# Transfer sizes and the gamma broadcast in a fused RMSNorm and swish kernel

## The chip, the core and the metric

The kernel runs on one core of one Trainium2 chip. The metric is the device time of the kernel in microseconds, the median over runs; less is better.

## The reference

```
def reference(x, gamma, eps):            # x: 16 x 1024 x 512 float32, gamma: 512
    rms = np.sqrt(np.mean(x ** 2, axis=-1, keepdims=True) + eps)
    x_norm = x / rms * gamma
    return (x_norm * (1.0 / (1.0 + np.exp(-x_norm)))).astype(np.float32)
```

Each of 16,384 rows of 512 numbers is divided by its root mean square, multiplied by gamma, and put through swish. 33.55 MB are read and as many written.

## The kernel before

The input is seen as 128 "rows per partition" of 512 numbers: 128 x 128 rows, and a row of all 128 partitions is 256 KB. A tile is a block of consecutive rows of the input, `sz` rows to each partition, so that each partition reads one run of `sz` x 2 KB from memory. The list `sizes` says how the 128 rows are cut into tiles. The tiles lie in one ring buffer `xb` of 96 rows per partition; the results are written over the input in the ring and are stored from there. A load that takes a place in the ring for the second time has to wait until the store of what lay there has landed.

The computation goes by chunks of `cn` = 4 rows (32 chunks in all), in a software pipeline written out by hand (`tc.manual_schedule()`: each engine runs its instructions in the order of the program):

- `sums(k)`: the sum of squares of each row, three rows on ACT (line 80), one on DVE (line 86).
- `root(k)`: mean plus eps on DVE (line 93), to the power -0.5 on POOL (line 97).
- `norm(k)`: row times its reciprocal root times gamma, four instructions on DVE (line 104).
- `swish(k)`: one ACT instruction over the chunk (line 111).

In turn k of the loop the order is `sums(k)`, `root(k)`, the stores whose last chunk was put through swish in turn k - 1 or before, `norm(k - 1)`, `swish(k - 2)`, and then the loads that have come due. So a chunk's swish stands on ACT behind the sums of two later chunks, and a tile's store behind the sums of its last chunk plus three.

Loads (line 70) are all issued from SP, in order, and nothing else is; 32 rows' worth of tiles is issued ahead of the loop. Stores (line 73) are issued from ACT's queue, between its activations. The framework gives every transfer one of eight completion semaphores in turn, and a transfer that gets a semaphore for the second time is issued only when the earlier transfer on it has landed.

Gamma is needed on all 128 partitions by `norm`. It is brought to partitions 0, 32, 64 and 96 by one transfer from ACT's queue into `gamma4` (line 116), which POOL has set to zero before (line 114), and a DVE shuffle (line 140) copies it within each group of 32 partitions into `gamma_sb`. The shuffle stands on DVE behind `root(0)`.

Of the kernel before, what the change touches and what calls it, by code (L numbers as in the profile page):

```python
# [1 line left out]

# [4 lines left out]


@with_exitstack
def kernel(  # L10
    ctx: ExitStack,
    tc: tile.TileContext,
    x: bass.AP,
    gamma: bass.AP,
    eps: bass.AP,
    out: bass.AP,
):
    nc = tc.nc
    P = nc.NUM_PARTITIONS
    AF = mybir.ActivationFunctionType  # L20
    ALU = mybir.AluOpType
    fp32 = mybir.dt.float32
    bf16 = mybir.dt.bfloat16

    xf = x.flatten_outer_dims()
    of = out.flatten_outer_dims()
    R, D = xf.shape


    sizes = [4, 4, 8] + [16] * 6 + [8, 8]  # L30
    ring = 96
    ahead = 32
    cn = 4
    n_act = 3
    N = sum(sizes)
    assert N * P == R, (N, R)


    tiles = []
    done = 0  # L40
    for sz in sizes:
        assert done % ring + sz <= ring
        tiles.append((done * P, sz, done % ring))
        done += sz
    chunks = [r for _, sz, at in tiles for r in range(at, at + sz, cn)]
    K = len(chunks)

    pool = ctx.enter_context(tc.tile_pool(name="all", bufs=1))
    junk_pool = ctx.enter_context(tc.tile_pool(name="junk", bufs=1))
    xb = pool.tile([P, ring, D], fp32, name="xb")  # L50
    gamma4 = pool.tile([P, D], fp32, name="gamma4")
    gamma_sb = pool.tile([P, D], fp32, name="gamma_sb")
    neg_half = pool.tile([P, cn], fp32, name="neg_half")
    ms = pool.tile([P, K, cn], fp32, name="ms")
    aeps = pool.tile([P, K, cn], fp32, name="aeps")
    rstd = pool.tile([P, K, cn], fp32, name="rstd")

    inv_d = 1.0 / float(D)
    eps_f = float(eps)

    def dram(ap, t):
        first, sz, _ = tiles[t]
        return ap[first : first + P * sz].rearrange("(p n) d -> p n d", n=sz)

    def buf(t):
        _, sz, at = tiles[t]
        return xb[:, at : at + sz, :]

    def load(t):
        nc.sync.dma_start(out=buf(t), in_=dram(xf, t))  # L70

    def store(t):
        nc.scalar.dma_start(out=dram(of, t), in_=buf(t))

    def sums(k):
        for j in range(cn):
            row = xb[:, chunks[k] + j, :]
            if j < n_act:
                junk = junk_pool.tile([P, D], bf16, name=f"junk_a{j}")
                nc.scalar.activation(  # L80
                    out=junk[:], in_=row, func=AF.Square,
                    accum_out=ms[:, k, j : j + 1],
                )
            else:
                junk = junk_pool.tile([P, D], bf16, name=f"junk_v{j}")
                nc.vector.tensor_tensor_reduce(  # L86
                    out=junk[:], in0=row, in1=row,
                    scale=1.0, scalar=0.0, op0=ALU.mult, op1=ALU.add,
                    accum_out=ms[:, k, j : j + 1],
                )  # L90

    def root(k):
        nc.vector.tensor_scalar(  # L93
            out=aeps[:, k, :], in0=ms[:, k, :], scalar1=inv_d, scalar2=eps_f,
            op0=ALU.mult, op1=ALU.add,
        )
        nc.gpsimd.tensor_tensor(  # L97
            out=rstd[:, k, :], in0=aeps[:, k, :], in1=neg_half[:], op=ALU.pow
        )

    def norm(k):
        for j in range(cn):
            row = xb[:, chunks[k] + j, :]
            nc.vector.scalar_tensor_tensor(  # L104
                out=row, in0=row, scalar=rstd[:, k, j : j + 1],
                in1=gamma_sb[:], op0=ALU.mult, op1=ALU.mult,
            )

    def swish(k):
        rows = xb[:, chunks[k] : chunks[k] + cn, :]  # L110
        nc.scalar.activation(out=rows, in_=rows, func=AF.Silu)  # L111

    with tc.manual_schedule():
        nc.gpsimd.memset(gamma4[:], 0.0)  # L114
        nc.gpsimd.memset(neg_half[:], -0.5)  # L115
        nc.scalar.dma_start(out=gamma4[0:P:32, :], in_=gamma.partition_broadcast(4))
        nc.scalar.preload_act_table_set("silu_and_others")  # L117

        loaded = 0
        rows_loaded = 0  # L120
        while rows_loaded < ahead:
            load(loaded)
            rows_loaded += tiles[loaded][1]
            loaded += 1

        ends = []
        e = 0
        for _, sz, _ in tiles:
            e += sz // cn
            ends.append(e)  # L130
        stored = 0
        for k in range(K + 3):
            if k < K:
                sums(k)
                root(k)
            while stored < len(tiles) and ends[stored] <= k - 2:
                store(stored)
                stored += 1
            if k == 0:
                nc.vector.stream_shuffle(gamma_sb[:], gamma4[:], [0] * 32)  # L140
            if 1 <= k <= K:
                norm(k - 1)
            if 2 <= k < K + 2:
                swish(k - 2)
                while loaded < len(tiles) and ends[loaded] <= k - 1 + ahead // cn + 2:
                    load(loaded)
                    loaded += 1


# [1 line left out]
_INS = ['x', 'gamma', 'eps']  # L151
_OUTS = [((16, 1024, 512), 'float32')]

_NUMBERS = {'eps': 9.999999747378752e-06}


# [26 lines left out]
```

## Time and profile before

| | us |
|---|---|
| Median of 3 runs (lowest, highest) | 163.08 (162.92, 163.41) |
| The profiled execution's own time | 162.92 |
| Its span in the trace | 161.1 |
| ACT busy | 118.7 (74% of the span) |
| DVE busy | 110.7 (69%) |
| POOL busy | 46.4 (29%) |
| Load queue (q1), time of its packets as a share of 16 engines | 49.1% |
| Store queue and gamma (q10), the same | 48.4% |

The span is the time from the first to the last instruction of the program in the trace; the time of a run has 1.8 us more around it. Queue q1 is that of the loads from SP, q10 that of ACT. A transfer is cut into packets, one for each run of memory, which are spread over the 16 DMA engines; the trace has a record of every packet with its queue, start, duration and size. Packets of 4 bytes are the completion marks, one for each DMA engine that takes part. The share of a queue is the sum of its packets' durations over 16 times the span.

### The profile page before, as it was taken

How to read it: one execution, taken by the hardware profiler on the slowest of the kernel's cores; microseconds unless marked ns; L12 is line 12 of the kernel's file. 1: busy time of each engine (PE TensorE's matmuls, PEld its weight loads, DVE VectorE, ACT ScalarE, POOL GpSimd, SP SyncE). 2: the span in 40 equal slices, each digit the busy share in tenths (PEclk: the TensorE clock that was granted, in tenths of full speed). 3: DMA queues.
4: the chain of work that ended last, by engine and by line, in shares of the span. 5: the costliest groups of instructions: out<-in, count | busy, mean ns of one | idle time of the engine just before them, and what ended most of it. 6: DMA issues, size and time to landing. Idle time of an engine off the chain costs nothing.

```text
span 161.1 us, 612 instructions
## 1 busy us (share of the span) xinstructions
DVE 110.7 (69%) x226; ACT 118.7 (74%) x225; POOL 46.4 (29%) x38
## 2 busy tenths in 40 slices
DVE  0376946998999999999966998069999604990000
ACT  3447919999999999999939996099999408954000
POOL 1052403333444433333333333033333302400000
DMA  5999989999899999999999999999999999999993
GB/s 171 437 435 521 390 352 488 413 403 480 366 407 431 484 411 447 399 456 447 399 447 456 399 439 464 417 415 421 431 435 464 419 403 472 415 415 423 439 415 146
DMA packets 3180, 67.15 MB, mean 417 GB/s; under 512 B 356, under 2 KB 356, under 8 KB 360
## 3 DMA queue, kind: packets, MB, share of 16 engines
q1 hardware_dynamic: 1584, 33.56, 49.1%
q10 hardware_dynamic: 1592, 33.56, 48.4%
q14 instruction: 4, 0.03, 0.0%
HBM read 33.56 MB, written 33.55 MB: 417 GB/s over the span
## 4 chain that ended last, share of the span: by engine, by line
DMA 59%; ACT 20%; another core or an unknown queue 4%; issue 4%; DVE 3%; SPq 1%; DVEq 0%; ACTq 0%
DMA xb<-in_x_dram 41%; DMA out_dram<-xb 19%; ACT junk_a L80 12%; ACT xb L111 8%; DVE xb L104 3%; SPq L70 1%; DVEq L178 0%; DVE aeps L93 0%; ACTq L80 0%
## 5 line engine op out<-in xcount | busy, mean ns | idle before, releaser
L104 DVE SCALAR_TENSOR_TENSOR xb<-xb,rstd,gamma_sb 128x512 f32<-128x512 f32 x128 | 87.4, 745 | 0.0
L80 ACT ACTIVATE junk_a<-xb 128x512 bf16<-128x512 f32 x96 | 59.0, 615 | 23.9 <-DMA xb<-in_x_dram 23.9
L97 POOL TENSOR_TENSOR rstd<-aeps,neg_half 128x4 f32<-128x4 f32 x32 | 45.6, 1426 | 94.1 <-DVE aeps L93 94.1
L111 ACT ACTIVATE xb<-xb 128x2048 f32<-128x2048 f32 x32 | 60.7, 1896 | 1.8 <-DVE xb L104 1.8
L86 DVE CUSTOM_DVE_ANT_0 junk_v<-xb 128x512 bf16<-128x512 f32 x32 | 21.9, 685 | 19.6 <-DMA xb<-in_x_dram 19.6
L80 ACT ACTIVATION_READ_ACCUMULATOR junk_a<-xb 128x1 f32 x96 | 18.0, 187 | 0.0
L93 DVE TENSOR_SCALAR aeps<-ms 128x4 f32<-128x4 f32 x32 | 5.4, 170 | 14.5 <-ACT junk_a L80 14.5
L117 ACT ACT_TABLE_LOAD x1 | 1.3, 1283 | 2.4 <-issue 2.4
L86 DVE DVE_READ_ACCUMULATOR2_ANT ms<- 128x1 f32 x32 | 2.6, 82 | 0.0
L140 DVE STREAM_SHUFFLE gamma_sb<-gamma 128x512 f32<-128x512 f32 x1 | 0.7, 725 | 0.0
L114 POOL MEMSET gamma<- 128x512 f32 x1 | 0.5, 524 | 0.3 <-POOLq L164 0.3
L164 POOL MEMSET const-float32-0.0<- 128x1 f32 x1 | 0.1, 98 | 0.2 <-issue 0.2
L164 POOL MEMSET const-bfloat16-1.0<- 128x1 bf16 x1 | 0.1, 101 | 0.0
L164 POOL MEMSET const-uint8-127<- 128x1 uint8 x1 | 0.1, 101 | 0.0
L115 POOL MEMSET neg_half<- 128x4 f32 x1 | 0.1, 101 | 0.0
L164 POOL MEMSET const-float32-1.0<- 128x1 f32 x1 | 0.1, 98 | 0.0
L140 DVE LOAD_MASK_SELECT gamma_sb<-gamma x1 | 0.0, 14 | 0.0
## 6 DMA issues: line engine op xcount, KB each, us to landing
xb<-in_x_dram SPq DMA_DIRECT2D x6, 4096.0 KB, 43.8
out_dram<-xb ACTq DMA_DIRECT2D x6, 4096.0 KB, 34.6
xb<-in_x_dram SPq DMA_DIRECT2D x3, 2048.0 KB, 38.8
out_dram<-xb ACTq DMA_DIRECT2D x3, 2048.0 KB, 13.9
xb<-in_x_dram SPq DMA_DIRECT2D x2, 1024.0 KB, 5.8
out_dram<-xb ACTq DMA_DIRECT2D x2, 1024.0 KB, 19.7
gamma<-in_gamma_dram ACTq DMA_DIRECT2D x1, 8.0 KB
```

The costliest lines, as they stand in the source:

```text
L70: nc.sync.dma_start(out=buf(t), in_=dram(xf, t))
L80: nc.scalar.activation(out=junk[:], in_=row, func=AF.Square, accum_out=ms[:, k, j : j + 1],)
L86: nc.vector.tensor_tensor_reduce(out=junk[:], in0=row, in1=row, scale=1.0, scalar=0.0, op0=ALU.mult, op1=ALU.add, accum_out=ms[:, k, j : j ...
L93: nc.vector.tensor_scalar(out=aeps[:, k, :], in0=ms[:, k, :], scalar1=inv_d, scalar2=eps_f, op0=ALU.mult, op1=ALU.add,)
L97: nc.gpsimd.tensor_tensor(out=rstd[:, k, :], in0=aeps[:, k, :], in1=neg_half[:], op=ALU.pow)
L104: nc.vector.scalar_tensor_tensor(out=row, in0=row, scalar=rstd[:, k, j : j + 1], in1=gamma_sb[:], op0=ALU.mult, op1=ALU.mult,)
L111: nc.scalar.activation(out=rows, in_=rows, func=AF.Silu)
L114: nc.gpsimd.memset(gamma4[:], 0.0)
L115: nc.gpsimd.memset(neg_half[:], -0.5)
L117: nc.scalar.preload_act_table_set("silu_and_others")
L140: nc.vector.stream_shuffle(gamma_sb[:], gamma4[:], [0] * 32)
L164: nc = _bacc.Bacc("TRN2", target_bir_lowering=False, num_devices=1)
```

## The change

Two things are changed. The list of tile sizes becomes two tiles of 4 rows (1 MB) and fifteen of 8 rows (2 MB); it was 4, 4, 8, six of 16 (4 MB), 8, 8. The ring, the chunks, the rows loaded ahead of the loop and the code of the loop stay. There are then 17 loads and 17 stores, where there were 11 of each. And gamma goes from memory to all 128 partitions by one transfer on ACT's queue, at the place of the former one; the buffer `gamma4`, its clearing on POOL and the shuffle on DVE are gone.

```
-    sizes = [4, 4, 8] + [16] * 6 + [8, 8]
+    sizes = [4, 4] + [8] * 15
...
-    gamma4 = pool.tile([P, D], fp32, name="gamma4")
...
-        nc.gpsimd.memset(gamma4[:], 0.0)
         nc.gpsimd.memset(neg_half[:], -0.5)
-        nc.scalar.dma_start(out=gamma4[0:P:32, :], in_=gamma.partition_broadcast(4))
+        nc.scalar.dma_start(out=gamma_sb[:], in_=gamma.partition_broadcast(P))
...
-            if k == 0:
-                nc.vector.stream_shuffle(gamma_sb[:], gamma4[:], [0] * 32)
```

## The prediction

> **What bounds the kernel now.** I read the page first: the DMA row of the 40 slices and the shares of the queues, then the chain.
>
> ```profile
> span 161.1 us, 612 instructions
> DVE 110.7 (69%) x226; ACT 118.7 (74%) x225; POOL 46.4 (29%) x38
> DMA  5999989999899999999999999999999999999993
> DMA packets 3180, 67.15 MB, mean 417 GB/s; under 512 B 356, under 2 KB 356, under 8 KB 360
> q1 hardware_dynamic: 1584, 33.56, 49.1%
> q10 hardware_dynamic: 1592, 33.56, 48.4%
> DMA 59%; ACT 20%; another core or an unknown queue 4%; issue 4%; DVE 3%; SPq 1%; DVEq 0%; ACTq 0%
> ```
>
> The two queues together take 97.5% of 16 engines' span, 157.1 of 161.1 us; ACT, the busiest engine, has 42 us to spare. The other 4.0 us lie mainly at the ends. Two kinds of window show it, and what packet size does:
>
> ```profile
> 0.00:1.70 1.70, 0.00 (x0) 0.00 (x0) 0.77 (x6) 1.00 0.00 0
> 60.00:100.00 40.00, 35.27 (x72) 36.67 (x71) 14.49 (x11) 1.00 1.00 433
> 133.20:140.40 7.20, 5.17 (x12) 6.67 (x14) 2.24 (x2) 1.00 1.01 437
> 150.10:155.00 4.90, 0.00 (x0) 0.00 (x0) 0.00 (x0) 1.00 1.00 428
> 159.90:161.10 1.20, 0.00 (x0) 0.00 (x0) 0.00 (x0) 1.00 0.00 0
> ```
>
> The last two columns are the busy share of the DMA engines and GB/s. Nothing moves before 1.7 us and after 159.9; with loads and stores mixed (60 to 100) the share is 1.00. While stores alone run, 4 MB transfers (32 KB packets) pass 437/1.01 = 433 GB/s, 2 MB ones (16 KB packets) 428. So the time is the work in the DMA engines plus some 3 us, and whatever an engine does earlier or later costs nothing as long as one queue has work. The waits of SP say the same:
>
> ```profile
> SPq L70 <- DMA out_dram<-xb: 55.9, 3, 27.1
> SPq L70 <- DMA xb<-in_x_dram: 19.6, 3, 15.3
> ```
>
> Loads were issued 75 us late in sum, for a place in the ring or a semaphore, and the engines were full all the same.
>
> **The work in packets.** The packet records have these medians: 9 ns for a 4-byte mark, 84 ns for 2 KB, 309 for 8 KB, 611 for 16 KB, 1213 for 32 KB. They follow each other without a gap on an engine. Each of 16 engines gets 8 packets and one mark of every transfer. Before, for each queue: 16 x 0.309 (two tiles of 4 rows) + 24 x 0.611 + 48 x 1.213 + 11 x 0.009 = 77.93 us; twice that, and 0.09 for gamma on four engines, is 155.9. The page's 157.1 has 1.2 us more: packets longer than the median, of which 0.4 us are in the first load, 0.5 at 19.5 to 22.9 us, where the first store's data begin (20.9), and 0.2 at 47.
>
> **Smaller tiles.** After, for each queue: 16 x 0.309 + 120 x 0.611 + 17 x 0.009 = 78.42 us. That is 0.49 more; for two queues +0.97 us. The reason is that two 16 KB packets take 1222 ns where one of 32 KB takes 1213, 96 times on each engine (0.86), and 12 more marks (0.11). Bounds: the windows above put it at 433/428, about 1%, of the some 117 us now spent in 32 KB packets, 1.3 us; taken as 433 against 431, which the rounding allows, 0.5. I take the packet medians, which rest on hundreds of packets. A gain is excluded here unless the longer packets go away; they may by up to 0.8 us (those after the first load), or one more start like that at 20 us may add 0.5.
>
> The Trainium skill, "DMA: Bandwidth & Descriptors", section "Anatomy of one DMA", speaks harder against the change: a fixed cost of about 2.0 us for a transfer, most of it waiting for the receipt. Paid in series, 12 more transfers would cost an estimated 24 us, and the sum would be 187 us. The trace disagrees for queued transfers: the marks of the last store but one came from 153.49 to 155.02 us, and in the window from 150.10 to 155.00, where the engines go over to the last store one by one, the share is 1.00; so a receipt is waited for beside the next transfer's data.
>
> **Gamma.** The four packets of 2 KB (360 less 356 in the page's counts) become 128. If they spread like a load's, that is 8 on each engine: 8 x 0.084 + 0.009 = 0.68 us, where engines 0 to 3 or their like had 0.09: +0.6 us, and it is in front of nothing that could hide it, since the loads fill the engines from 1.7 us on. Bounds: the four old packets read the same 2 KB at nearly the same time (starts 5.54 to 5.61) and each took 84 ns, so I take 84; sixteen readers may be slower, at most like an 8 KB packet, 8 x 0.309 = 2.5 us (+2.4). All on four engines, as before, would be 32 x 0.084 = 2.7 us (+2.6). Nothing is the lower bound, if the engine that ends last gets none.
>
> Who waits for it: `norm(0)` on DVE. Before:
>
> ```profile
> 7.52 0.17 DVE L93 TENSOR_SCALAR aeps<-ms 128x4 f32<-128x4 f32 x1 [1.28 <-ACT junk_a L80]
> 7.63 0.72 DVE L140 STREAM_SHUFFLE gamma_sb<-gamma 128x512 f32<-128x512 f32 x1
> 8.25 0.67 DVE L86 CUSTOM_DVE_ANT_0 junk_v<-xb 128x512 bf16<-128x512 f32 x1
> 10.15 2.73 DVE L104 SCALAR_TENSOR_TENSOR xb<-xb,rstd,gamma_sb 128x512 f32<-128x512 f32 x4
> 12.98 0.63 ACT L80 ACTIVATE junk_a<-xb 128x512 bf16<-128x512 f32 x1 [2.94 <-DMA xb<-in_x_dram]
> ```
>
> The first gamma packet moved at 5.54 us. Eight packets in turn with the load's of 0.309 to 0.611 us end at 5.54 + 8 x 0.084 + 7 x 0.309 + 0.611, about 9.0, and land some 0.4 later; `norm(0)` begins at 10.15, behind `root(1)`, and the load before it comes 0.6 us later too. So it waits for nothing new, and if it did, DVE's next work (12.92, with the third load) has little behind it: until 20.9 us only loads move. The shuffle (0.72 us on DVE), the clearing (0.52 on POOL) and the dependence on them save nothing for the same reason: `norm(0)` follows `root(1)` at 10.07, whatever the shuffle does. ACT's issue of the transfer (1.09 us before, at 1.29) lies ahead of its first sums at 5.54; doubled, it would still.
>
> **Does a queue always hold work afterwards?** SP's 17 issues are behind nothing but each other; of ACT's 6 more, 0.34 us each, ACT's spare 42 us carry the 2.0. Eight semaphores with loads and stores in turn allow about four of each in flight, so a load waits for the fourth before it, and the load queue never runs out. Stores: ACT does a chunk (1 MB) in 3.64 us (14.96 to 18.60 in the timeline), a tile in 7.3; with equal packets each queue gets half, so a 2 MB store takes 2 x 4.9 = 9.8 us and ACT keeps up. The loads' end: some 18.5 us of load work is done when stores begin at 20.9; two 1 MB stores with 8 KB packets take 4.9 us of the engines and the loads beside them 9.8, which gives 35.6; the remaining 50 us of load work at half rate end at about 136. Some 23 us of store work is left then. Before, the last load landed at 133.65 and the last store was issued at 146.78, 13.1 us later; after 13.1 us, 23 - 4.9 - 13.1 = 5 us of other stores are still to go. So the last store joins a busy queue, and the end is set by the work.
>
> **Sum.** 0.97 + 0.6 = 1.6 us. The profiled execution's own time 162.92 becomes 164.5; it is the lowest of three, 0.16 under the median, so I add to the median: 164.7.
>
> **The rivals.**
> 1. The tail becomes ACT's (12%, slower by more). A store whose turn of semaphore falls on a load that is not there yet stops ACT's queue, with the sums and swishes behind it, or the store backlog is worked off by 136 us. Then, after the last load, the stores of the last three tiles wait for 13.1 us of ACT and only the last one's 4.9 us is left: against three stores in a row (14.7 us) 3 to 7 us are lost; 167 to 172. It decides once the 5 us of cover above are gone. For it: each tile's store now stands behind the second next tile's first sums. Against: ACT's 42 us.
> 2. The change costs nothing that shows (8%): the 0.8 us of longer packets and half of the spread of the engines at the end (marks of the last store from 158.35 to 159.88) go with the 32 KB packets, 163.1 to 163.5.
> 3. Faster (7%). In the stretch from 20 to 46 us the store queue has 8 KB packets against the loads' 32 KB; equal packets let the engines finish together. If the whole spread of 1.5 us and the 0.8 us go, 2.3 is taken off 1.6: 162.4. It needs gamma at its cheapest too. Against: the shares of 1.00.
> That the change does not do what it says would show in the counts: 1920 packets of 16 KB for each queue and 128 of 2 KB.
>
> **The numbers.** Slower with the sum as given 73%. A measurement can tell about 0.3%, 0.5 us, from no change: slower by more 85% (the forecast and rival 1), within 8%, faster 7%. The range runs from 163.4 (0.8 us of longer packets and 0.5 of the spread gone) to 166.6 (163.08 + 0.97 + 2.6, gamma at its dearest); rivals 3 and 1 are left out but for their edges.
>
> **What would show it.** Right: a share of both queues together of about 158.5 us, DMA slices at 9 until the end, packets of 2 KB at 84 ns, an end of the last packet about 1.6 us later. Wrong: slices under 9 after 140 us (rival 1), 2 KB packets of several hundred ns, `norm(0)` waiting for gamma past 13 us, or a sum of both queues that has not grown.

## The result and the profile after

The changed kernel takes 164.78 us (median of four runs, 164.69 to 164.88) against 163.12 for the kernel before: 1.66 us more, a ratio of 1.010 with a 95% interval of 1.0083 to 1.0118. The forecast was 164.7. The total was right, in part by luck: of the terms of its sum one was right, one was too small by a factor of three, and a third, which the sum had put at nothing, made up for about half of that.

The page of the kernel after, parts 1 to 3:

```profile
span 163.1 us, 627 instructions
DVE 109.8 (67%) x224; ACT 118.8 (73%) x225; POOL 45.9 (28%) x37
DMA  5999999999999999999999999999999999999992
DMA packets 5044, 67.41 MB, mean 413 GB/s; under 512 B 560, under 2 KB 560, under 8 KB 688
q1 hardware_dynamic: 2448, 33.56, 48.9%
q10 hardware_dynamic: 2592, 33.82, 48.7%
```

The engines for DMA are full from 1.7 us to the end, as before. The two queues hold 97.6% of 163.1 us, 159.2 us of work, 2.1 more than before. 688 less 560 are the 128 packets of gamma. So the loss is work in the DMA engines. Where it is shows in the same two windows of both kernels (a row has the stretch and its length, the busy time of DVE, ACT and POOL, the clock, the busy share of the DMA engines and GB/s), here first before, then after:

```profile
1.70:12.00 10.30, 4.04 (x11) 5.17 (x13) 2.45 (x2) 1.00 1.00 408
12.00:40.00 28.00, 22.17 (x46) 23.68 (x47) 8.63 (x6) 1.00 1.00 424
```

```profile
1.70:12.00 10.30, 1.65 (x6) 4.64 (x13) 1.01 (x1) 1.00 1.00 361
12.00:40.00 28.00, 25.35 (x52) 25.18 (x49) 11.21 (x8) 1.00 1.01 430
```

In the first 12 us the changed kernel moves 47 GB/s less in the mean; from 12 to 40 us it moves 6 more, although its packets are smaller. The engines count as busy in both, so a lower rate means packets that take longer. The timeline of ACT gives the size of the early loss: the sums of the third tile, which before started at 12.98 us (the last row of the timeline in the prediction), wait for their load until 14.82:

```profile
14.82 0.63 ACT L79 ACTIVATE junk_a<-xb 128x512 bf16<-128x512 f32 x1 [2.94 <-DMA xb<-in_x_dram]
```

That is 1.84 us, where the forecast had 0.6 for gamma. From the third load's landing to the last store's both kernels take 147.3 us (12.90 to 160.24, 14.74 to 162.05), where the forecast had 1.0 us more for the smaller tiles. Two theories went into the experiments. Theory A: the terms are right as forecast, and their places are an accident. Theory B: gamma carries the whole loss, and the smaller tiles cost nothing in the end.

### The profile page after: what moved, and what is told of

It reads as the page before. It is cut to its first block, busy times and chain, and to the rows that moved or that the text cites. A ratio compares the mean times of both kernels' runs of the same rounds, so it can differ in the third digit from the quotient of the medians.

```text
span 163.1 us, 627 instructions
## 1 busy us (share of the span) xinstructions
DVE 109.8 (67%) x224; ACT 118.8 (73%) x225; POOL 45.9 (28%) x37
## 4 chain that ended last, share of the span: by engine, by line
DMA 48%; ACT 35%; issue 5%; DVE 3%; another core or an unknown queue 1%; SPq 0%; ACTq 0%; DVEq 0%
DMA xb<-in_x_dram 37%; ACT junk_a L79 19%; ACT xb L110 16%; DMA out_dram<-xb 11%; DVE xb L103 3%; SPq L69 0%; ACTq L72 0%; DVEq L174 0%; DVE aeps L92 0%; ACTq L79 0%
## 5 line engine op out<-in xcount | busy, mean ns | idle before, releaser
L110 ACT ACTIVATE xb<-xb 128x2048 f32<-128x2048 f32 x32 | 60.7, 1898 | 23.6 <-DMA xb<-in_x_dram 21.8
```

## The experiments

Each run was made on one chip together with the kernel before, and the median of the kernel before on that chip is given with it; the ratio and its 95% interval follow. Numbers from a trace are from one profiled execution of each kernel.

**One half at a time.** The first run has the sizes of before and the new gamma:

```
-    sizes = [4, 4] + [8] * 15
+    sizes = [4, 4, 8] + [16] * 6 + [8, 8]
```

> The tile sizes of before, gamma by its own broadcast to 128 partitions. Theory A (the terms of the forecast as they were written): gamma costs 0.6 us, so 163.12 + 0.6 = 163.7. Theory B (read from the trace of the changed kernel: its third load lands at 14.74 us where that of before landed at 12.90, and from there both take 147.3 us more): gamma carries the whole loss, 1.8 us, so 164.9. Third load's landing, by A 13.5, by B 14.7.

Measured: 164.24 (before 163.02; ratio 1.0069, 1.0051 to 1.0087), +1.2. The third load lands at 14.82.

The second has the new sizes and the gamma of before (four partitions and the shuffle).

> The tile sizes of the changed kernel, gamma as before by four partitions and a shuffle. Theory A: the smaller packets cost 1.0 us, 164.1. Theory B: the 1.0 us of smaller packets is given back by the packets over the median after the first load, of which before had 0.8 us and the changed kernel 0.1, so 163.1 to 163.3.

Measured: 163.95 (before 163.02; 1.0053, 1.0035 to 1.0072), +0.93. For the tiles theory A is right and B falls: by themselves they cost what the packets say. For gamma neither is right: 1.8 us are lost early, but only 1.2 are left at the end. The same windows, of gamma alone and of sizes alone:

```profile
1.70:12.00 10.30, 1.58 (x6) 4.64 (x13) 1.01 (x1) 1.00 0.94 355
12.00:40.00 28.00, 22.55 (x46) 22.11 (x43) 10.10 (x7) 1.00 1.02 439
```

```profile
1.70:12.00 10.30, 4.03 (x11) 5.17 (x13) 2.46 (x2) 1.00 1.01 408
12.00:40.00 28.00, 25.29 (x52) 26.98 (x54) 10.08 (x7) 1.00 1.00 415
```

Both marks of the changed kernel, the slow start and the faster stretch behind it, come with the broadcast: 355 and then 439 GB/s with it, 408 and then 415 without. The packets over the median account for the second window. What the packets started between 12 and 50 us took beyond the median of their size (where it was over 20 ns), summed and divided by the 16 engines, is 0.73 us in before and 0.81 with the sizes alone, but 0.06 with the broadcast, with either sizes. In the first window the loss has two forms: in the changed kernel the engines are busy (1.00) and the packets take longer, with gamma alone the share is 0.94, so that about 0.5 us of the same delay is idle time of the engines.

**Why the broadcast is dear at the start.** Two changes to the changed kernel:

```
-        nc.scalar.dma_start(out=gamma_sb[:], in_=gamma.partition_broadcast(P))
+        nc.scalar.dma_start(out=gamma_sb[:], in_=xf[0:P, :])
```

> The changed kernel, but the transfer into gamma_sb reads 128 different rows of x in place of gamma's one row (so rows are scaled by wrong numbers); bytes, packets and place are the same. If the broadcast is dear because 16 engines read one and the same 2 KB at a time, its packets fall to about 84 ns and the time to 164.78 - 1.2 = 163.6. If it is dear for being 128 small packets in the engines' first microseconds, whatever they read, nothing changes: 164.8.

Measured: 164.48 (before 163.02; 1.0083, 1.0064 to 1.0102). The end moved by 0.3 us only (128 distinct rows cost 0.53 on top of the sizes alone, the one row 0.7 to 0.8), but the place of the loss moved as the reading of one row says: the third load lands at 13.76 us, 1.0 earlier, and the packets take 84 ns. (Their length alone would not show it: with gamma alone, which reads one row, their mean is 85 ns and the third load is as late as in the changed kernel.) What was won at the start was lost behind it: the packets over the median are back (0.66 us between 12 and 50 us).

```profile
1.70:12.00 10.30, 2.65 (x8) 4.64 (x13) 1.84 (x2) 1.00 0.97 404
12.00:40.00 28.00, 25.33 (x52) 26.16 (x52) 10.71 (x8) 1.00 1.00 418
```

The other:

```
+        nc.gpsimd.memset(gamma_sb[:], 0.0)
         nc.gpsimd.memset(neg_half[:], -0.5)
```

> The changed kernel, with gamma_sb cleared on POOL first, so that the broadcast is issued after the clearing, behind the first loads, as the four-partition transfer of before was (issue at 1.29 us in place of 0.73, first packet then expected near 5.5 us in place of 2.3). If the collision with the first load's ramp is what makes it dear, its packets take about 84 ns and the time is 163.6; if it is the reading of one row by 16 engines, 164.8 as it is, with the delay moved from the first load to the second.

Measured: 164.75 (before 163.02; 1.0100, 1.0081 to 1.0120). The first gamma packet moved at 5.21 us, the second load took the delay (its last packet ends at 9.42 us, in before at 7.59), and the time is the same. So it is not the ramp, the start of the first load; with the run before, the reading of one row is what is left.

**Packet size by itself**, three times as strong, with gamma as before:

```
-    sizes = [4, 4, 8] + [16] * 6 + [8, 8]
+    sizes = [4] * 32
```

> The kernel before with 32 tiles of 4 rows (1 MB, 8 KB packets), gamma as before: the price of small packets by itself, three times as large. If each packet costs its 9 ns on a full engine: 256 x 0.309 + 32 x 0.009 = 79.4 us for each queue against 77.9, for both +2.9: 166.0. If the larger count of transfers cost a fixed time each (the 21 more of each kind), far more: over 170. If small packets cost nothing that shows, 163.1.

Measured: 173.21 (before 163.17; 1.0615, 1.0595 to 1.0634): more than the packets cost, and not for a fixed time of each transfer. Its DMA slices and two windows:

```profile
DMA  5999999999999999999999999999999877656786
```

```profile
40.00:120.00 80.00, 38.96 (x82) 45.27 (x85) 16.31 (x12) 1.00 1.01 427
140.00:165.00 25.00, 23.44 (x47) 23.18 (x42) 8.64 (x6) 1.00 0.72 298
```

While both queues are full, 8 KB packets pass 427 GB/s, where from 40 to 100 us the kernel before passes 432 and the changed kernel 431: the packets' price is there and small. Most of the other 7 us is rival 1 of the forecast. The loads are through at 121 us; from 132 on the share falls, and what is left goes at the pace of ACT, 1 MB in 3.64 us, which is 288 GB/s. Its waits say why ACT was late (us in total, times, the longest):

```profile
ACT xb L111 <- DMA xb<-in_x_dram: 39.6, 9, 9.7
```

A swish (line 111) needs no load. What stood ahead of it on ACT's queue was a store whose completion semaphore belonged to a load still under way; nine times the whole queue stood still behind such a store. ACT's spare time went there, and the backlog of stores was gone some 11 us after the loads ended.

**The broadcast among full queues**, added to the kernel before:

```
+            if k == 12:
+                nc.scalar.dma_start(out=gamma4[:], in_=gamma.partition_broadcast(P))
```

> The kernel before, with one more transfer: gamma broadcast to 128 partitions into gamma4 from ACT's queue in turn 12, after the shuffle, where nobody reads it again. It shows what such a transfer costs among full queues of loads and stores. By its packets at 84 ns: +0.7 us, 163.7. By what the first loads lost in the changed kernel (their third landing 1.8 us later): +1.8, 164.9.

Measured: 164.00 (before 163.17; 1.0049, 1.0032 to 1.0066), +0.83, near the 0.7 of the packets. All took 84 to 89 ns. They ran among packets of 1.2 us, and the 128 reads were spread over 9.6 us (79.56 to 89.20); in the changed kernel they were spread over 4.5 (2.34 to 6.80). The added transfer also shifts the turn of the semaphores, and the last load lands at 124.06 us where before had 133.65; the engines stay full, so this changes no work.

**What takes the longer packets away?** Six kernels that add one small transfer to the kernel before. First, 16 partitions, one packet on each engine, from gamma and then from x (`xf[0:16, :]` in its place), ahead of everything on ACT's queue:

```
+        nc.scalar.dma_start(out=gamma_sb[0:P:8, :], in_=gamma.partition_broadcast(16))
         nc.gpsimd.memset(gamma4[:], 0.0)
```

> The kernel before, with one more small transfer ahead of all others on ACT's queue: gamma's 2 KB to 16 partitions of gamma_sb (one packet on each of 16 engines), overwritten later by the shuffle. In the runs with the full broadcast the packets over the median at 18 to 38 us (0.8 us of every engine in before and in the run with the sizes alone) are absent. If what takes them away is that every engine has once worked for ACT's queue, or once read gamma, they go here too, at a price of 0.1 us: 162.4 to 162.6. If it is that the full broadcast spreads the engines in time (marks of the third load 0.24 us apart without it, 0.56 with it), one packet each changes nothing: 163.2.

> As the run before, but the 16 packets read 16 rows of x and not gamma's. If having once worked for ACT's queue is enough, the same 162.4 to 162.6. If gamma itself must have been read by every engine, the longer packets stay and the time is 163.2. If the spread of the engines is the cause, 163.2 as well, as in the run before.

Measured: 163.20 and 163.28 (before 163.17; 1.0000, 0.9987 to 1.0012, and 1.0007, 0.9997 to 1.0017). The longer packets stay: 0.61 and 0.75 us. A first use of the queue by every engine is not it. Nor is the spread of the engines in time: the marks of the third load are 0.55 us apart in the run with x and 0.54 in that with distinct rows, as far as with the broadcast (0.56), and both keep the longer packets.

Then 256 bytes of gamma to all 128 partitions, and a first write to the output:

```
+        nc.scalar.dma_start(out=gamma_sb[:, 0:64], in_=gamma[0:64].partition_broadcast(P))
         nc.gpsimd.memset(gamma4[:], 0.0)
```

```
+        nc.scalar.dma_start(out=of[R - 16 : R, :], in_=gamma4[1:P:8, :])
         nc.scalar.preload_act_table_set("silu_and_others")
```

> The kernel before, with one more transfer ahead of the others on ACT's queue: the first 64 numbers of gamma (256 bytes) to all 128 partitions of gamma_sb, overwritten later by the shuffle. It has the packets of the full broadcast, 8 on each engine and all from one place in memory, at an eighth of the bytes. If reading gamma eight times with every engine is what takes away the longer packets at 18 to 48 us (present with one packet per engine, absent with the full broadcast), they go here at a price of some 0.2 us: 162.4 to 162.7. If it takes the full broadcast's delay of the first loads, or anything else, they stay: 163.3 to 163.5.

> The kernel before, with one more small transfer on ACT's queue behind gamma's: 16 partitions of zeros (one packet of 2 KB on each of 16 engines) into 16 rows of the output, which the last store overwrites. If the longer packets where the first stores begin are a price of each engine's first write to the output, they move to the first microseconds and are gone at 18 to 23 us; the time is 162.7 if they overlap with the first load's start, 163.2 if they only move. If they have another cause, they stay where they are: 163.2 to 163.3.

Measured: 164.32 (before 163.09; 1.0073, 1.0061 to 1.0085) and 163.09 (1.0005, 0.9996 to 1.0014). The write moved nothing (0.80 us of longer packets). The short broadcast is the clearest run of all. It has an eighth of gamma's bytes and costs the same 1.2 us:

```profile
1.70:12.00 10.30, 2.16 (x8) 5.17 (x13) 1.01 (x1) 1.00 0.95 340
12.00:40.00 28.00, 22.53 (x46) 22.12 (x43) 10.07 (x7) 1.00 1.02 438
```

The third load lands at 14.82 us, as with the full 2 KB; the 128 reads were spread over 4.5 us (2.56 to 7.10), as in the changed kernel (with gamma alone over 3.8, 3.06 to 6.88); and the longer packets are gone (0.05). So what the early broadcast costs goes with its number of reads of one place and not with its bytes. (No run reads 128 distinct places of 256 bytes, so at that size the number of packets and the one place are not told apart.) My expectation had priced it by its bytes, at 0.2 us, and missed the other 1.0.

Last, the same with fewer partitions (32 here, then `gamma_sb[0:P:2, 0:64]` with 64), to see whether the gain can be had without the loss:

```
+        nc.scalar.dma_start(out=gamma_sb[0:P:4, 0:64], in_=gamma[0:64].partition_broadcast(32))
```

> As the run with 256 bytes of gamma to 128 partitions ahead of the rest, but to 32 partitions: two reads by each of 16 engines. If the early loss is a fixed time for each read of one place (1.9 us for 128), it is 0.5 us here. If the longer packets at 18 to 48 us go away whenever many engines have read one place at a time, the time is 163.1 + 0.5 - 0.7 = 162.9; if that takes the long queue of 128 reads, they stay and the time is 163.6.

> The same to 64 partitions, four reads by each engine: early loss 1.0 us; 163.4 if the longer packets go away, 164.0 if they stay.

Measured: 163.33 (before 163.22; 1.0006, 0.9993 to 1.0020) and 163.61 (1.0023, 1.0011 to 1.0034). With 32 reads the time can't be told from before, with 64 it is longer: in neither does the gain outrun the loss. Nor do the reads go at one fixed rate: the 32 took 0.40 us (4.86 to 5.26), the 64 took 1.31 (4.72 to 6.04), 128, begun at about the same time in the run with the later broadcast, took 4.1 (5.21 to 9.33). Side by side, in us:

| gamma transfer in the first microseconds | third load lands | longer packets, 12 to 50 us |
|---|---|---|
| before | 12.90 | 0.73 |
| sizes alone | 12.94 | 0.81 |
| + 16 distinct rows of x | 13.08 | 0.75 |
| + 16 reads of gamma | 13.25 | 0.61 |
| + 32 reads of 256 bytes | 13.21 | 0.58 |
| + 64 reads of 256 bytes | 14.04 | 0.32 |
| + 128 reads of 256 bytes | 14.82 | 0.05 |
| gamma alone, 128 reads of 2 KB | 14.82 | 0.06 |
| changed kernel | 14.74 | 0.06 |
| changed, broadcast issued later | 14.64 | 0.06 |
| changed, 128 distinct rows | 13.76 | 0.66 |

Why the longer packets around the first stores shrink as many engines read one place at the start stays open. It goes with the number of such reads in all the runs above; a first use of the queue, a first write to the output and the spread of the engines are ruled out as causes. The delay itself is not: no run holds up the first loads by as much without such reads, and the delay of 0.9 us by distinct rows leaves 0.66 us of longer packets. No run beat the kernel before.

## Why the prediction was right

**What bounds it: right.** DMA slices at 9 to the end, and whatever moved on the compute engines cost nothing: the shuffle, the clearing and 0.9 us of DVE are gone without a trace in the total (the run with 256 bytes keeps shuffle and clearing and loses the same 1.2 us as gamma alone). The two queues' work was to be 158.5 us (157.1 and the 1.6 of the sum make 158.7) and is 159.2.

**Smaller tiles, +0.97: right.** +0.93 by themselves. The medians of 16 KB packets are 611 ns in every run that has them. Twelve more transfers, and 42 more in the run with 1 MB tiles while its queues were full, cost their packets. The fixed 2.0 us of a transfer that the Trainium skill gives ("DMA: Bandwidth & Descriptors", "Anatomy of one DMA") were not paid in series in any run; that section gives them for transfers issued from GpSimd, and all transfers here are issued from SP and ACT.

**Gamma, +0.6: this term was mis-sized.** It cost 1.2 us with the old sizes and 0.7 on top of the new (1.66 less 0.93), made of 1.84 us lost at once and some 0.7 got back. I had taken 84 ns for each packet because four readers at nearly the same time had shown no delay. With 16 readers the packets' mean is 117 ns (up to 284), and the packets of the load queue beside them grew too: 8 KB loads took 387 ns in the mean against 335 before. On each engine that is 0.93 us for gamma's own packets and 0.83 for the loads'. My bounds, nothing to 2.6 us, held the total, but the working priced gamma's packets alone: what they do to the loads beside them had no term. With gamma alone the same delay came about otherwise: packets of 85 ns in the mean, loads of 369, and some 0.5 us of idle engines.

**The longer packets, taken as unchanged (0 of -0.8 to +0.5): wrong.** Some 0.7 us of them went, which the bounds allowed. I tied them to the 32 KB packets of the old tiles in rival 2; the run with sizes alone keeps them (0.81), so it is not the tiles.

Made from the profiled executions, the sum is now 0.97 + 1.84 - 0.67 = 2.1, where their own times differ by 1.9 (162.92 to 164.83). Two errors of some 1.2 and 0.7 us, one up and one down, left a total that looks better than its working: that it fell on the forecast is luck.

**Who waits for gamma: right in effect, wrong in detail.** I had the first packet at 5.54 us; it moved at 2.34, because the transfer no longer waits for POOL's clearing (issue at 0.73 in place of 1.29; with a clearing put back, 5.21), and collided with the first load. `norm(0)` did not wait:

```profile
11.92 0.17 DVE L92 TENSOR_SCALAR aeps<-ms 128x4 f32<-128x4 f32 x1 [1.34 <-ACT junk_a L79]
12.01 2.74 DVE L103 SCALAR_TENSOR_TENSOR xb<-xb,rstd,gamma_sb 128x512 f32<-128x512 f32 x4
```

Gamma had landed at 7.44.

**The cover of the tail: right, and nearer to its end than it looked.** I had the last load at 136 us and 5 us of other stores to go when the last store is issued. The last load landed at 134.2, the last store was issued at 152.17, and the store before it landed at 157.22: 5 us. But the way there was another: 17.9 us passed between the last load's landing and the last store's issue, where I had taken 13.1 from before. Rival 1's mechanism did happen. In the waits of the changed kernel, and at its first place in the timeline of ACT:

```profile
ACT xb L110 <- DMA xb<-in_x_dram: 21.8, 4, 10.2
```

```profile
61.12 0.34 ACTq L72 DMA_DIRECT2D out_dram<-xb  x1
61.50 1.91 ACT L110 ACTIVATE xb<-xb 128x2048 f32<-128x2048 f32 x1 [8.15 <-DMA xb<-in_x_dram]
```

The store at 61.12 is issued when the load that held its semaphore lands (61.04). Four such stops took 21.8 of the 42 us that ACT had to spare, and the engines were full all the while. With 1 MB tiles nine stops took 39.6, and the tail fell to ACT. So rival 1 was a matter of size, not of kind.

**Rivals 2 and 3.** Equal packets did not let the engines end together: the marks of the last store come from 159.71 to 161.72, 2.0 us apart, where before had 1.5.

## What to carry to other kernels

When the DMA engines are full from end to end, price a change by its packets (their medians times their number on each engine), and look at the compute engines only for the point at which the queues run dry. Transfers of 2 MB in place of 4 MB cost 0.6% of the time here; those of 1 MB were dear less for their packets than because each needs a semaphore and a place in an in-order queue. A broadcast from memory to all partitions at the start of this kernel cost by the number of its reads of one place, in the middle of the stream by its packets; which of the differences between the two places makes this so was not tried. The transfer to four partitions of before costs four packets of 84 ns, and the shuffle on an idle engine nothing that shows.

## What was not expected of the hardware

- 128 reads of one place by 16 engines took 3.8 to 4.5 us at the start, some 28 to 33 in a microsecond, whether they were 256 bytes or 2 KB long, and the loads on the same engines were held up with them; 32 such reads took 0.40 us and 64 took 1.31. 128 distinct rows at the same place in the program took 3.3 us and delayed the third load by 0.9 in place of 1.8.
- In the kernels without such reads, some 45 to 85 load packets, most of them near the first stores, take up to 0.6 us longer (0.7 to 0.8 us for each engine in the mean between 12 and 50 us); with 128 reads of one place at the start that disappears. The cause was not found.
- A sum of terms measured one at a time did not add up: +1.2 for gamma and +0.9 for the sizes, +1.7 together; the intervals of the three ratios, 0.2% to each side, are wide enough to hold the difference.
